# Seven block products for the last eight gate and up slices of layer 0's second half

## The chip, the cores and the metric

The kernel runs on one core of one Trainium2 chip. The metric is the device time of one execution in microseconds; the number to beat or to miss is the median of several executions.

## The reference

One inference step of a decoder with two layers, for 1024 prompt tokens and 8 sample tokens that share all weights. Cut to what matters here:

```python
def swiglu(h, w_gu, w_down):
    gate, up = jnp.split(h @ w_gu, 2, axis=-1)
    return (jax.nn.silu(gate) * up) @ w_down

# in run_trunk, per layer (layer 0: mixer A, layer 1: mixer B)
    h = h + rmsnorm(mix, g[1])
    h = h + rmsnorm(swiglu(rmsnorm(h, g[2]), w_gu[l], w_down[l]), g[3])
```

The model width is 1024 and the hidden width of the feed-forward network is 2816, 22 slices of 128. `w_gu` holds gate and up side by side. Results are wanted in float32 precision.

## The kernel before

The tokens are worked in two halves: g = 0 has 512 prompt tokens, g = 1 has 512 prompt tokens and the 8 sample tokens, 520 columns. Activations are kept transposed, 128 features by tokens. A float32 product is three matmuls: weights and activations are each split into a rounded high part and the rest (`split_w` and `split_to`: ScalarE casts, VectorE subtracts), and high x high, high x low and low x high are added up in PSUM. A half of 520 columns goes through TensorE as two pieces of 260, each with its own weight load.

`proj` is such a product for one slice of 128 outputs: for each of eight row blocks of 128 it issues 3 matmuls for each piece of 260, so 48 for the second half. `ffn.part(pi)` works through one of five groups of slices (`PARTS`: 5, 5, 4, 4 and 4). For each slice it runs `proj` for gate, `silu` (VectorE clips, ScalarE does exp, ln, exp, VectorE multiplies), `proj` for up, a multiplication and a split; then eight down projections over the group's slices add to the residual tile R.

The last stage of the program, layer 1's feed-forward for the second half (`ffn_w`), works otherwise. There gate and up of a slice are seen together as a 2 x 2 block matrix (rows 0 to 511 and 512 to 1023 of the weights; gate and up) times two blocks of 260 columns, and are got from seven products of 512 x 128 by 512 x 260 in place of eight, with sums of activations (`sums_w`) and sums of weight blocks. `gate_up_w` runs the seven products of one slice into four accumulators pa, pb, pc and pd; between products ScalarE copies one accumulator, negated, into another, and VectorE adds and subtracts (`gt`). It uses ScalarE's Silu itself, which lies in another table than exp and ln. The weight sums are made in DRAM by `weight_sums`: eight transfers a group, issued on GpSimd's queue, some of them accumulating, each held back by a token (a ScalarE copy of one column, then a GpSimd copy), so that they are spread over time.

Tiles come from pools with a fixed number of buffers: `wraw` (5) and `wspl` (5) for raw and split weights, `bpool` (7) for attention's temporary tiles, `apool` (8), `cpool` (4), and in PSUM `mmp` (2 tiles of 2 banks), `smp` (3 banks) and `nsp` (1). The main program weaves generators together by step counts, and the tile framework then sets each engine's order by its own estimate of when operands are ready. SP's queue carries the weight loads in one order, GpSimd's queue the sums and the gathers of cached keys and values.

The stages that the prediction speaks of, by the times of the trace: layer 0's first memory attention and output projection (some 240 to 350 us), the first half's `f0.part(4)` of layer 0 (some 765 to 835), the second half's parts 2, 3 and 4 of layer 0 (1191 to 1396), the second attention of layer 1 (some 1520 to 1935), its output projection (1935 to 1984), and layer 1's blocked feed-forward (2098 to 2382).

Of the kernel before, what the change touches and what calls it, by code (L numbers as in the profile page):

```python
# [24 lines left out]
def tile_decoder(  # L25
# [167 lines left out]
    def sv(ap, g):  # L193
        return ap[:, :G] if g == 0 else ap.rearrange("p (a n) -> p a n", a=2)

    def split_w(W, k0, nk, m0):
        out = []
        for a in range(0, nk, 4):
            n = min(4, nk - a)
            raw = wraw.tile([P, 4, P], F32, tag="w", name=nm("w"))  # L200
            nc.sync.dma_start(
                raw[:, :n, :],
                W[(k0 + a) * P : (k0 + a + n) * P, m0 : m0 + P].rearrange("(k p) m -> p k m", p=P),
            )
            ws = wspl.tile([P, 2, 4, P], F32R, tag="ws", name=nm("ws"))
            nc.scalar.copy(ws[:, 0, :n, :], raw[:, :n, :])  # L206
            nc.vector.tensor_sub(ws[:, 1, :n, :], raw[:, :n, :], ws[:, 0, :n, :].bitcast(F32))  # L207
            for i in range(n):
                out.append((ws[:, 0, i, :], ws[:, 1, i, :]))
        return out  # L210
# [90 lines left out]

    def sums_w(xs, ops):

# [27 lines left out]

    def YT():
        return xpool.tile([P, 2, NG[1]], F32R, tag="x0", name=nm("y"))
# [172 lines left out]

    def gate_up_w(l, f, ops, spl, raws, pair=None):

# [14 lines left out]
        def split(src):  # L523
            w = spl()
            nc.scalar.copy(w[:, 0, :], src)  # L525
            nc.vector.tensor_sub(w[:, 1, :], src, w[:, 0, :].bitcast(F32))  # L526
            return w

# [10 lines left out]

        pa, pb, pc, pd = (Q(i) for i in range(4))  # L540
        product(pa, 0, True)
# [88 lines left out]
    htok, done = [], []  # L630

    PARTS = [(0, 5), (5, 5), (10, 4), (14, 4), (18, 4)]

    class ffn_w:


        def __init__(self, l, x, plain):
            self.g, self.l, self.x, self.ops, self.plain, self.n, self.r, self.pi = 1, l, x, [], plain, 0, 0, 0
            self.R = self.acc = None
            self.half, self.mids = [], {}  # L640
            self.sums = sums_w(x, self.ops)

# [22 lines left out]
        def gate_up(self, pi, j0=0, j1=None):  # L665
# [3 lines left out]
            for j in range(j0, nf if j1 is None else j1):  # L669
                self.pi = pi  # L670
                if f0 + j < self.plain:
                    mt, ins = gate_up_q(l, f0 + j, self.x)
                    mids.append(mt)
                    with tc.issue_after(ins.ins):
                        for _ in range((1, 2, 1, 0)[j]):
                            next(self.sums, None)
                else:
                    pair = pairs[j // 2] if self.block(pi) and j < 4 else None
                    mids.append(gate_up_w(l, f0 + j, self.ops, self.spl, self.raws, pair))
                yield  # L680
# [214 lines left out]
    class ffn:  # L895
        def __init__(self, g, l, xt, rows=False):
            self.g, self.l, self.xt, self.rows = g, l, xt, rows
            self.R = self.acc = None

        def part(self, pi):  # L900
# [4 lines left out]
            mids = []  # L905
            for j in range(nf):
                pg = proj(g, w_gu[l], 0, ND, (f0 + j) * P, self.xt)
                sg = silu(None, pg, g)
                pu = proj(g, w_gu[l], 0, ND, DFF + (f0 + j) * P, self.xt)
                nc.vector.tensor_mul(sv(sg, g), sv(sg, g), pv(pu, g))  # L910
# [3 lines left out]
                self.now = sg[:, 0:1]  # L914
                yield
            if pi == 0:
                self.R = R_one()
            if last:
                self.acc = small([P, WID], tag="st", bufs=3)
            for m in range(ND):  # L920
                ps = proj(g, w_down[l], f0, nf, m * P, mids)
                evac_raw(g, self.R, ps, m, self.acc, pi == 0, last)
                self.now = self.R[m][:, 0:1]
                if m % 2:
# [844 lines left out]
    for blk in range(2):  # L1769
# [25 lines left out]
    weave((a1.core(), 22), (f0.part(0), 9), (down_sums(1, (1, 2, 3), lambda: f0.now), 24))  # L1795
    a1.open()
# [74 lines left out]
```

## Time and profile before

| | before |
|---|---|
| median of 3 runs | 2419.36 us (2418.62 to 2421.4) |
| the profiled execution | 2420.43 us, its span 2418.7 us |
| TensorE matmuls busy | 2395.5 us, 15411 instructions |
| weight loads busy | 2132.5 us |
| VectorE busy | 1602.8 us |
| ScalarE busy | 1241.3 us |
| GpSimd busy | 140.5 us |
| moved by DMA | 369.25 MB, 153 GB/s in the mean |
| stage 1191 to 1403 us | 212 us: TensorE 212.00, VectorE 105.11, ScalarE 85.84 busy; DMA share 0.83, 215 GB/s |

The engines are named PE (TensorE), PEld (its weight loads), DVE (VectorE), ACT (ScalarE), POOL (GpSimd) and SP (the queue that issues most loads). A row's "L220" is line 220 of the kernel. "Idle before <- X" says what ended the idle time in front of an instruction. PE's busy time is modelled and can reach its whole stretch without the array being at its peak, so it is read together with what PE waited for.

### The profile page before, as it was taken

The numbers are of one execution on the slowest core, as the hardware profiler recorded it, in microseconds if no ns is written. First come the engines' busy times: TensorE is split into PE (matmuls) and PEld (weight loads), VectorE is DVE, ScalarE is ACT, GpSimd is POOL, SyncE is SP. The second block draws the span as 40 slices with busy tenths as digits, with TensorE's granted clock in tenths as the row PEclk, the third lists the DMA queues.
The fourth block names the chain that finished last, engine by engine and source line by source line (L and its number), as shares of the span: only waits on it lengthen the run. The fifth ranks groups of instructions, "written<-read, shape, count | busy, mean of one in ns | idle before, by whom it ended". The sixth has DMA issues, their size and how long they took to land.

```text
span 2418.7 us, 40898 instructions
## 1 busy us (share of the span) xinstructions
PE 2395.5 (99%) x15411; PEld 2132.5 (88%) x15411; DVE 1602.8 (66%) x2792; ACT 1241.3 (51%) x2472; POOL 140.5 (6%) x215
## 2 busy tenths in 40 slices
PE   8999999999999999999999999999999999999998
PEld 6888998888877888999999989887787797999998
DVE  5777566765865677555544585877687648857885
ACT  5558554544444445555433454555454445565665
POOL 3000001200000000011111100121000000000000
PEclk9999999999999999999999999999999999999999
DMA  6353255884733445456778966644453334365652
GB/s 188 103 163 106 73 159 141 193 217 131 217 109 96 135 150 183 123 134 151 183 196 215 245 181 200 190 135 124 131 182 93 95 119 126 121 191 176 182 175 75
DMA packets 499224, 369.25 MB, mean 153 GB/s; under 512 B 19757, under 2 KB 444314, under 8 KB 499026
## 3 DMA queue, kind: packets, MB, share of 16 engines
q1 hardware_dynamic: 476008, 307.87, 42.7%
q0 software_dynamic: 22912, 58.73, 10.4%
q8 instruction: 121, 1.98, 0.3%
q14 instruction: 77, 0.63, 0.1%
q10 hardware_dynamic: 106, 0.04, 0.0%
HBM read 336.74 MB, written 80.15 MB: 172 GB/s over the span
## 4 chain that ended last, share of the span: by engine, by line
PE 91%; issue 4%; DVE 3%; ACT 1%; DMA 0%; POOL 0%; SPq 0%; DVEq 0%; POOLq 0%; ACTq 0%
PE mm L220 63%; PE q L535 7%; PE q L714 2%; PE q L493 2%; PE mm L1225 2%; PE s L1064 1%; PE q L778 1%; PE s L1023 1%; PE s L1408 1%; PE mm L977 1%; PE mm L1000 1%; PE q L862 1%; PE s L1583 1%; PE s L1622 1%; PE s L1050 1%
## 5 line engine op out<-in xcount | busy, mean ns | idle before, releaser
L220 PE MATMUL mm<-x,ws 128*128 128x260 f32 (+1 forms) x7776 | 1327.0, 329 | 0.5 <-DVE x L228 0.3
L220 PEld LDWEIGHTS mm<-x,ws 128*128 128x128 f32 x7776 | 1148.6, 188 | 140.1 <-issue 3.2
L206 ACT CAST ws<-w 128x512 fp32r<-128x512 f32 (+1 forms) x672 | 398.0, 593 | 648.2 <-PE mm L220 561.6
L207 DVE TENSOR_TENSOR ws<-w,ws 128x512 fp32r<-128x512 f32 (+1 forms) x672 | 438.2, 656 | 222.3 <-ACT ws L206 213.2
L220 PE MATMUL mm<-m,ws 128*128 128x512 f32 (+1 forms) x2112 | 391.0, 342 | 0.0
L220 PEld LDWEIGHTS mm<-m,ws 128*128 128x128 f32 x2112 | 323.5, 188 | 45.5 <-issue 2.1
L526 DVE TENSOR_TENSOR ws<-w,ws 128x512 fp32r<-128x512 f32 x126 | 86.6, 691 | 46.6 <-ACT ws L525 44.4
L535 PE MATMUL q<-y,ws 128*128 128x260 f32 x864 | 112.9, 283 | 0.0
L535 PEld LDWEIGHTS q<-y,ws 128*128 128x128 f32 x864 | 107.5, 188 | 0.0
L426 DVE TENSOR_TENSOR r<-r,mm 128x512 f32<-128x512 f32 (+1 forms) x96 | 66.0, 688 | 59.5 <-PE mm L220 58.1
L525 ACT CAST ws<-w 128x512 fp32r<-128x512 f32 x126 | 77.8, 618 | 47.7 <-PE q L535 15.3
L260 DVE TENSOR_SCALAR t<-mm 128x512 f32<-128x512 f32 (+1 forms) x74 | 51.2, 692 | 60.8 <-PE mm L220 60.7
L264 DVE TENSOR_TENSOR t<-t,t 128x512 f32<-128x512 f32 (+1 forms) x66 | 45.8, 693 | 68.1 <-ACT t L263 68.1
L910 DVE TENSOR_TENSOR t<-t,mm 128x512 f32<-128x512 f32 (+1 forms) x66 | 45.4, 689 | 67.4 <-PE mm L220 67.3
L535 PE MATMUL q<-x,ws 128*128 128x260 f32 x648 | 86.7, 283 | 0.0
L535 PEld LDWEIGHTS q<-x,ws 128*128 128x128 f32 x648 | 81.7, 189 | 0.0
L621 POOL COPY mk<-rr 128x1 f32<-128x1 f32 x64 | 29.6, 462 | 735.3 <-ACT rr L620 735.3
L290 DVE TENSOR_TENSOR st<-st,n 128x512 f32<-128x512 f32 (+1 forms) x91 | 62.2, 691 | 2.7 <-ACT n L289 1.5
L227 ACT CAST m<-t 128x512 fp32r<-128x512 f32 (+1 forms) x76 | 47.4, 624 | 26.0 <-DVE t L910 19.5
L261 ACT ACTIVATE t<-t 128x512 f32<-128x512 f32 (+1 forms) x66 | 42.1, 637 | 34.1 <-DVE t L260 29.9
L1161 POOL DMA_INDIRECT c<-in_cache_sb_k,pidx x16 | 20.0, 1250 | 608.9 <-DMA out_sbv_prompt<-c 427.2
L228 DVE TENSOR_TENSOR m<-t,m 128x512 fp32r<-128x512 f32 (+1 forms) x76 | 52.6, 692 | 2.3 <-ACT m L227 1.1
(385 smaller groups left out, 2889.2 us busy)
## 6 DMA issues: line engine op xcount, KB each, us to landing
w<-in_w_gu SPq DMA_DIRECT2D x334, 256.0 KB
w<-in_w_down SPq DMA_DIRECT2D x156, 256.0 KB
w<-in_w_in_a SPq DMA_DIRECT2D x80, 256.0 KB
wsum<-in_w_gu POOLq DMA_DIRECT2D x18, 1024.0 KB, 9.4
w<-wsum SPq DMA_DIRECT2D x72, 256.0 KB
w<-in_w_o SPq DMA_DIRECT2D x64, 256.0 KB
dsum<-in_w_down POOLq DMA_DIRECT2D x18, 512.0 KB, 6.6
w<-in_w_mem_kv SPq DMA_DIRECT2D x32, 256.0 KB
```

The costliest lines, as they stand in the source:

```text
L206: nc.scalar.copy(ws[:, 0, :n, :], raw[:, :n, :])
L207: nc.vector.tensor_sub(ws[:, 1, :n, :], raw[:, :n, :], ws[:, 0, :n, :].bitcast(F32))
L220: nc.tensor.matmul(ps[:, a, : PW[g]], wt, xt[k][:, xi, o : o + PW[g]], start=(k == 0 and wi == 0), stop=(k == nk - 1 and wi == 2),)
L228: nc.vector.tensor_sub(dst[1], src, dst[0].bitcast(F32))
L260: nc.vector.tensor_scalar(sv(x, g), pv(ps, g), -44.0, None, op0=ALU.max)
L290: nc.vector.tensor_add(acc[:, :n], acc[:, :n], t[:, :n])
L426: nc.vector.tensor_add(dst, dst, pv(ps, g))
L493: nc.tensor.matmul(pp[a][:, :h], wt, xt[k][:, xi, a * h : (a + 1) * h], start=(k == 0 and wi == 0), stop=(k == ND - 1 and wi == 2),)
L525: nc.scalar.copy(w[:, 0, :], src)
L526: nc.vector.tensor_sub(w[:, 1, :], src, w[:, 0, :].bitcast(F32))
L535: nc.tensor.matmul(ps[:, :h], w[:, wj, k * P : (k + 1) * P], x[:, xi, :], start=(first and k == 0 and wi == 0), stop=(k == 3 and wi == 2), ...
L714: nc.tensor.matmul(acc[i][q][:, :h], w[:, wj, o : o + P], x[:, xi, :], start=(first and t == 0 and wi == 0), stop=(t == 1 and wi == 2), sk ...
```

## The change

The second half's feed-forward of layer 0 runs slices 14 to 21 (parts 3 and 4, `FIRST = 14`) through `gate_up_w`. Its four accumulators come from the pools that are open there: pa and pd from `smp`, pb and pc as the two halves of one `mm` tile. Raw block weights lie in `bpool`, split ones in `wspl` and `cpool`, the sums of activations in `apool`. The sums are made beside slices 10 to 12. Silu's table is loaded in slice 14, and exp's and ln's again before part 4's down projection.

The weight sums for the two groups (16 transfers) are issued early: 7 while the first memory attention of layer 0 runs, 5 in the output projection behind it, 4 in `f0.part(4)`. Of layer 1's 40 transfers 16 stay where they were, 10 (24 before) stay beside the second half's parts 2 to 4, 8 go beside the second attention of layer 1 and 6 beside its output projection. The token now reads the newest split weight tile (`now`) in place of `sg` or R.

```diff
+        def quads(self):
+            two = mmp.tile([P, 2, 512], F32, tag="mm", name=nm("mm"))
+            return S(), two[:, 0, :], two[:, 1, :], S()
...
             for j in range(nf):
+                if f0 + j >= self.plain:
+                    mids.append(gate_up_w(
+                        l, f0 + j, self.ops, self.spl,
+                        lambda: B()[:, :512].rearrange("p (k m) -> p k m", m=P), self.quads,
+                    ))
+                    yield
+                    continue
                 pg = proj(g, w_gu[l], 0, ND, (f0 + j) * P, self.xt)
...
+                with tc.issue_after(ins.ins):
+                    for _ in range({4: 1, 3: 2, 2: 1}.get(self.plain - f0 - j, 0) if self.plain < NF else 0):
+                        next(self.sums)
                 yield
...
+            if last and self.plain < NF:
+                with tc.issue_after(done[-1].ins):
+                    nc.scalar.preload_act_table_set("natural_log_exp_and_others")
...
-    weave((a0.mem(), 8), (a1.fq(), 8))
+    here = lambda: now[0]
+    ws = weight_sums(0, (3, 4), here)
+    weave((a0.mem(), 8), (a1.fq(), 8), (islice(ws, 7), 7))
     o0 = out_proj(0, 0, M)
-    drain(o0.mm(a0.xo))
+    weave((o0.mm(a0.xo), 8), (islice(ws, 5), 5))
...
-    drain(f0.part(4))
+    weave((f0.part(4), 8), (ws, 4))
...
-    f1 = ffn(1, 0, o1.x)
-    ws = weight_sums(1, range(5), lambda: f1.now, 4)
+    f1 = ffn(1, 0, o1.x, FIRST)
+    ws = weight_sums(1, range(5), here, 4)
     weave((chain(b0.sb(), b0.mem()), 24), (chain(f1.part(0), f1.part(1)), 18), (islice(ws, 16), 17))
-    weave((chain(f1.part(2), f1.part(3), f1.part(4)), 24), (ws, 24))
+    weave((chain(f1.part(2), f1.part(3), f1.part(4)), 24), (islice(ws, 10), 10))
...
+        (chain(iter(range(20)), islice(ws, 8)), 32),
     )
     o1 = out_proj(1, 1, A, True)
-    drain(o1.mm(b1.xo))
+    weave((o1.mm(b1.xo), 8), (ws, 6))
```

What this does to the order, at three places. First TensorE at slice 14. Before, the gate projection of the slice stands there as one run: eight row blocks `x`, six matmuls each, into one `mm` tile:

```order
L220 MATMUL mm_12721<-x_9192,ws_12713 128x260 x6
L220 MATMUL mm_12721<-x_9196,ws_12713 128x260 x6
L220 MATMUL mm_12721<-x_9236,ws_12713 128x260 x6
L220 MATMUL mm_12721<-x_9240,ws_12713 128x260 x6
L220 MATMUL mm_12721<-x_9281,ws_12718 128x260 x6
```

Now, from the end of product 4 of slice 14 (into pb) to the start of product 6; `mm_12867` holds pb and pc, `s_13005` and `s_13006` are pa and pd of slice 15:

```order
L539 MATMUL mm_12867<-a_12454,ws_12944 128x260 x3
L539 MATMUL s_13005<-x_9280,ws_13009 128x260 x3
L539 MATMUL s_13005<-x_9284,ws_13009 128x260 x3
L539 MATMUL s_13005<-x_9324,ws_13009 128x260 x3
L539 MATMUL s_13005<-x_9328,ws_13009 128x260
L539 MATMUL mm_12867<-x_9369,ws_12965 128x260 x3
L539 MATMUL mm_12867<-x_9373,ws_12965 128x260 x3
L539 MATMUL mm_12867<-x_9413,ws_12965 128x260 x3
L539 MATMUL mm_12867<-x_9417,ws_12965 128x260 x3
L539 MATMUL s_13005<-x_9328,ws_13009 128x260 x2
L539 MATMUL s_13006<-a_12122,ws_13027 128x260 x3
L539 MATMUL mm_12867<-a_12121,ws_12983 128x260 x6
```

Ten matmuls of slice 15 have moved in front of product 5 (`x_9369` and on) and five in front of product 6 (`a_12121`). The first matmul of product 5 waits for VectorE, as does the first of product 6.

Second, SP's queue near the start of part 3, where the block weights (`b`, two of gate or up and then sums) and the loads of the down projections (`w`) now share it:

```order
L523 DMA b_13007<-in_w_gu 128x4x128
L523 DMA b_13025<-wsum_2332 128x4x128
L203 DMA w_13420<-in_w_down 128x4x128
L523 DMA b_13042<-wsum_2333 128x4x128
L203 DMA w_13451<-in_w_down 128x4x128
L203 DMA w_13487<-in_w_down 128x4x128
L523 DMA b_13060<-in_w_gu 128x4x128
```

The loads of part 3's down projection, `w_13420` and on, have moved between the block weights of slice 15, since the five tiles of `wraw` are free while gate and up use `bpool`.

Third, GpSimd's queue behind the stage. Before, the last sums of layer 1 stood in front of the remaining gathers of keys:

```order
L624 DMA wsum_13649<-in_w_gu 512x512
L621 COPY mk_14274<-rr_14272 128x1
L626 DMA wsum_13651<-wsum_13649 512x512
L621 COPY mk_14347<-rr_14345 128x1
L624 DMA wsum_13651<-in_w_gu 512x512
L1161 DMA c_16438<-in_cache_sb_k,pidx 128x512 x2
```

Now the moved sums (here the first of the 14) come behind the last gather of values:

```order
L1191 DMA c_17516<-in_cache_sb_v,pidx 128x512 x2
L1191 DMA c_17627<-in_cache_sb_v,pidx 128x512 x2
L1191 DMA c_17715<-in_cache_sb_v,pidx 128x512 x2
L625 COPY mk_18463<-rr_18461 128x1
L628 DMA wsum_14233<-in_w_gu 512x512
```

The sums have moved from ahead of the gathers to behind all of them, and the first gathers of keys, which before stood ahead of all of layer 1's sums, now come after the eighth of the ten sums that stay beside this stage.

More of the change, by code (lines that the diff above doesn't have):

```diff
@@ L194, in sv @@
         return ap[:, :G] if g == 0 else ap.rearrange("p (a n) -> p a n", a=2)
+    now = [None]
     def split_w(W, k0, nk, m0):
@@ L207, in split_w @@
             nc.vector.tensor_sub(ws[:, 1, :n, :], raw[:, :n, :], ws[:, 0, :n, :].bitcast(F32))
+            now[0] = ws[:, 0, 0, 0:1].bitcast(F32)
             for i in range(n):
@@ L505, in gate_up_q, with gate_up_w @@
         return mt, last
-    def gate_up_w(l, f, ops, spl, raws, pair=None):
+    def gate_up_w(l, f, ops, spl, raws, quads, pair=None):
         h, n = PW[1], NG[1]
@@ L526, in split @@
             nc.vector.tensor_sub(w[:, 1, :], src, w[:, 0, :].bitcast(F32))
+            now[0] = w[:, 0, 0:1].bitcast(F32)
             return w
@@ L538, in product @@
                     )
-        pa, pb, pc, pd = (Q(i) for i in range(4))
+        pa, pb, pc, pd = quads()
         product(pa, 0, True)
@@ L630, in tile_decoder @@
     htok, done = [], []
+    FIRST = 14
     PARTS = [(0, 5), (5, 5), (10, 4), (14, 4), (18, 4)]
@@ L640, in __init__ @@
             self.half, self.mids = [], {}
-            self.sums = sums_w(x, self.ops)
+            self.sums = sums_w(x, self.ops, Y0)
         def spl(self):
@@ L678, in gate_up @@
                     pair = pairs[j // 2] if self.block(pi) and j < 4 else None
-                    mids.append(gate_up_w(l, f0 + j, self.ops, self.spl, self.raws, pair))
+                    mids.append(gate_up_w(
+                        l, f0 + j, self.ops, self.spl, self.raws, lambda: [Q(i) for i in range(4)], pair
+                    ))
                 yield
@@ L895, in tile_decoder, with __init__, spl @@
     class ffn:
-        def __init__(self, g, l, xt, rows=False):
-            self.g, self.l, self.xt, self.rows = g, l, xt, rows
+        def __init__(self, g, l, xt, plain=NF):
+            self.g, self.l, self.xt, self.plain = g, l, xt, plain
             self.R = self.acc = None
+            self.ops, self.n = [], 0
+            self.sums = sums_w(xt, self.ops, lambda: A(F32R))
+        def spl(self):
+            self.n += 1
+            if self.n % 8 in (1, 4, 6):
+                return cpool.tile([P, 2, 512], F32R, tag="c", name=nm("ws"))
+            return wspl.tile([P, 2, 512], F32R, tag="ws", name=nm("ws"))
+        def quads(self):
+            two = mmp.tile([P, 2, 512], F32, tag="mm", name=nm("mm"))
+            return S(), two[:, 0, :], two[:, 1, :], S()
         def part(self, pi):
@@ L1789, in tile_decoder @@
     weave((chain(a0.gate(), a0.merge()), 8), (start(1, x1), 14))
-    weave((a0.mem(), 8), (a1.fq(), 8))
+    here = lambda: now[0]
+    ws = weight_sums(0, (3, 4), here)
+    weave((a0.mem(), 8), (a1.fq(), 8), (islice(ws, 7), 7))
     o0 = out_proj(0, 0, M)
-    drain(o0.mm(a0.xo))
+    weave((o0.mm(a0.xo), 8), (islice(ws, 5), 5))
     weave((o0.finish(), 17), (chain(a1.v(), a1.qm(A)), 8))
     f0 = ffn(0, 0, o0.x)
-    weave((a1.core(), 22), (f0.part(0), 9), (down_sums(1, (1, 2, 3), lambda: f0.now), 24))
+    weave((a1.core(), 22), (f0.part(0), 9), (down_sums(1, (1, 2, 3), here), 24))
     a1.open()
```

10 lines of the change are left out of this document (5 added, 5 removed).

## The prediction

> **What bounds the kernel now.** I read the page first, then the waits of PE, then the chain that ended last, then PE's timeline around the changed stage.
>
> ```profile
> span 2418.7 us, 40898 instructions
> PE 2395.5 (99%) x15411; PEld 2132.5 (88%) x15411; DVE 1602.8 (66%) x2792; ACT 1241.3 (51%) x2472; POOL 140.5 (6%) x215
> ```
>
> PE is busy 99% of the span, but its ends are modelled, so this alone proves little. The view of PE's waits does better: engine and line, what they waited for, total us, times, longest.
>
> ```profile
> PE s L145 <- DMA prow<-in_hg_norm: 7.7, 1, 7.7
> PE s L1610 <- DVE b L1604: 3.0, 9, 0.5
> ...
> PE mm L977 <- DVE memt L228: 0.2, 1, 0.2
> ```
>
> These are ten rows whose totals add up to about 15 us, half of it before the first matmul. In the chain of waits (start, duration, engine, line, count) the stage that the change touches is one unbroken row, and so are the stages of layer 1 that already run the block products (L535):
>
> ```profile
> 1191.49 209.81 PE mm L220 x1730
> ...
> 2143.56 50.48 PE q L535 x420
> ...
> 2290.64 40.42 PE q L535 x336
> ```
>
> So here PE alone sets the time: a matmul taken out of this stage is worth its whole pace, as long as nothing new makes PE wait. Everything else is either hidden or becomes such a wait.
>
> **The matmuls.** PE's timeline in the stage (start, duration, count):
>
> ```profile
> 1257.66 46.09 PE L220 MATMUL mm<-x,ws 128*128 128x260 f32 x384
> 1303.60 23.20 PE L220 MATMUL mm<-m,ws 128*128 128x260 f32 x192
> 1326.64 46.09 PE L220 MATMUL mm<-x,ws 128*128 128x260 f32 x384
> 1372.56 23.20 PE L220 MATMUL mm<-m,ws 128*128 128x260 f32 x192
> ```
>
> The x384 rows are gate and up of slices 14 to 17 and 18 to 21 (4 slices of 96 matmuls). From start to start they take 1303.60 - 1257.66 = 45.94 and 1372.56 - 1326.64 = 45.92 us, 119.6 ns a matmul. Afterwards a slice has 7 products x 4 x 3 = 84 matmuls of the same 260 columns, 336 for four slices. The chain's last L535 row is that very thing: four slices, 336 matmuls, 40.42 us (120.3 ns each). Each part gains 45.93 - 40.42 = 5.5 us, both parts **11.0 us**. The other new PE work is nil: the operand sums are made on DVE and ACT.
>
> **Waits that the shared PSUM tile adds.** In layer 1 the accumulators pb and pc have banks of their own. Here they are the two halves of one `mm` tile, and in the new order the first matmul of product 5 (into pc) waits for DVE, as the first of product 6 (into pb) does: the former for L557, which reads pb, the latter for L559, which reads pc. The order fills the two places with 8 to 10 and with 5 matmuls of the next slice (or of the down projection). How long must a fill be? One slice of layer 1, on PE, DVE and ACT (what is L557, L559 and L561 now was L553, L555 and L557 there):
>
> ```profile
> 2306.36 1.59 PE L535 MATMUL q<-y,ws 128*128 128x260 f32 x12
> 2307.79 1.61 PE L535 MATMUL q<-x,ws 128*128 128x260 f32 x12
> 2309.24 1.62 PE L535 MATMUL q<-y,ws 128*128 128x260 f32 x12
> ```
>
> ```profile
> 2307.55 0.69 DVE L526 TENSOR_TENSOR ws<-w,ws 128x512 fp32r<-128x512 f32 x1 [0.65 <-ACT ws L525]
> 2308.16 0.42 DVE L553 TENSOR_TENSOR t<-t,q 128x260 f32<-128x260 f32 x1
> 2308.64 0.69 DVE L526 TENSOR_TENSOR ws<-w,ws 128x512 fp32r<-128x512 f32 x1
> 2309.43 0.43 DVE L555 TENSOR_TENSOR t<-q,t 128x260 f32<-128x260 f32 x1
> ```
>
> ```profile
> 2309.96 0.42 ACT L557 ACTIVATE n<-t 128x260 f32<-128x260 f32 x1
> ```
>
> Product 5's slots end at 2309.24; L555 starts at 2309.43, ends at 2309.86, and the instruction that waits for it starts at 2309.96: 0.72 us from the last slot to the release. Five matmuls cover 0.60, so 0.12 us stays open per slice. Product 4's slots end at 2307.79; L553 starts 0.37 later behind a split, plus 0.42 and 0.10: 0.89 us, covered by 0.96 to 1.20. With one more split of 0.69 in front it would be 1.58, and 0.38 stays open; I take a fifth of that, 0.07. Together 0.19 us x 8 slices = **1.5 us**. The ends: nothing, and with no cover at all (0.72 + 0.89) x 8 = 12.9 us.
>
> **Supply of the block products.** Busy time in stretches (span; PE, PEld, DVE, ACT, POOL; granted clock, DMA share, GB/s), first of the changed stage, third of layer 1's four slices:
>
> ```profile
> 1191.00:1237.00 46.00, 46.00 (x385) 45.94 (x384) 22.54 (x33) 20.99 (x37) 6.76 (x9) 1.00 0.61 166
> 1367.00:1378.00 11.00, 11.00 (x93) 11.00 (x93) 6.13 (x9) 5.76 (x10) 1.58 (x2) 1.00 1.09 305
> 2290.00:2331.00 41.00, 41.00 (x343) 41.00 (x342) 31.60 (x63) 26.72 (x58) 0.00 (x0) 1.00 0.61 183
> ```
>
> In layer 1 the same products leave DVE 31.60 and ACT 26.72 busy of 41.00, with PE never idle; the new slices have less DVE work (no sums for a blocked down projection). The weights need 7 x 256 KB in 10.1 us, 182 GB/s, and ten weight sums of 1 MB over some 200 us add 51: 233 GB/s. Before, PE went on unhindered at 305 GB/s and a DMA share of 1.09. I cost the supply at **nothing**. Its cover is depth: 7 raw tiles and 9 split tiles. For a whole raw tile's round 7 x 1.44 = 10.1 us is allowed:
>
> ```profile
> L526 DVE TENSOR_TENSOR ws<-w,ws 128x512 fp32r<-128x512 f32 x22 | 15.2, 692 | 7.7 <-ACT ws L525 7.3
> L525 ACT CAST ws<-w 128x512 fp32r<-128x512 f32 x21 | 13.0, 617 | 5.9 <-PE q L535 3.4 <-ACT ws L525 1.1 <-PE q L714 0.8
> ```
>
> ```profile
> wsum<-in_w_gu POOLq DMA_DIRECT2D x18, 1024.0 KB, 9.4
> ...
> wsum<-in_w_gu POOLq DMA_DIRECT2D x6, 256.0 KB, 4.8
> ```
>
> Cast and split take 1.3 us; the nearest transfer of 256 KB whose landing the page shows takes 4.8. 6.1 us fits.
>
> **Operand sums.** Per pair of k: 12 DVE and 4 ACT instructions of 260 columns, four times.
>
> ```profile
> L563 DVE TENSOR_TENSOR n<-n,n 128x260 f32<-128x260 f32 x4 | 1.7, 424 | 0.0
> L227 ACT CAST ys<-n 128x260 fp32r<-128x260 f32 x6 | 2.5, 409 | 1.4 <-DVE n L563 1.3
> ```
>
> 48 x 0.424 = 20.4 us of DVE, 16 x 0.409 = 6.5 of ACT, in part 2, where DVE is idle 23 of 46 us while gate and up run. Nothing, while that holds. If the largest group (two pairs, 10.2 us) stood whole ahead of the DVE instruction that frees an `mm` bank, PE would use up the other bank's 48 x 0.120 = 5.7 us and wait 4.4. I take 0.
>
> **Silu's table.** Two table loads are added on ACT, one in slice 14, one before part 4's down projection.
>
> ```profile
> L765 ACT ACT_TABLE_LOAD x1 | 1.3, 1283 | 0.0
> ```
>
> 2 x 1.28 = 2.6 us if bare; split tiles stand eight products (11 us) ahead, so 0. The Trainium skill (ScalarE: Activation LUTs, What ACT_TABLE_LOAD costs) counts a drain of about 1.38 us on top, 2.66 a switch; by it a bare pair would cost 5.3 us instead of 2.6, and the sum is the same while the splits are ahead. The row here shows no idle time before the load.
>
> **Weight sums.** Sixteen POOL transfers are new (12 while layer 0's first memory attention and output projection run, 4 beside the first half's last part); of layer 1's 40, 14 move from this stage to the second attention of layer 1 (8) and to its output projection (6).
>
> ```profile
> 300.00:345.00 45.00, 44.93 (x274) 39.58 (x273) 25.58 (x41) 20.84 (x38) 0.00 (x0) 1.00 0.56 171
> 765.00:835.00 70.00, 70.00 (x329) 57.78 (x328) 38.91 (x57) 31.68 (x52) 0.00 (x0) 1.00 0.41 124
> 1935.00:1984.00 49.00, 49.00 (x388) 47.42 (x387) 16.65 (x25) 20.27 (x37) 0.00 (x0) 1.00 0.42 130
> ```
>
> Five in 45 us add 117 to 171 GB/s, four in 70 add 60 to 124, six in 49 add 128 to 130: at most 288, under the 305 that cost PE nothing. The gathers of cached keys now stand behind this stage's blocks, since both use the pool `cpool`, but in the new order all gathers of values come before the moved sums on POOL. If PE had to sit out all 30 transfers at 305 GB/s, it would be 30 x 3.4 = 103 us; the row at share 1.09 lies nearest, so 0. The sums' tokens are ACT copies of one column:
>
> ```profile
> L620 ACT COPY rr<-t x36: 184/187/192, 391.1 to 1374.0; 128x1 f32<-128x1 f32 x36
> ```
>
> Sixteen more are 3 us of an ACT that is half idle; reading a weight split instead of `sg` or R, they wait for no other engine.
>
> **Sum.** 2420.43 us (the profiled execution) - 11.0 + 1.5 = 2410.9. The median of the runs shown, 2419.36, lies 1.07 lower: **2409.9, said as 2410**.
>
> **Rivals.** First, *the fills don't cover*: DVE gets late in its queue, and products 5 and 6 wait. For it: the first matmuls of both name DVE, and DVE has splits of 0.69 us on both sides of L557 and L559. Against: the fills match the latencies above to a tenth. Bare, it gives 2419.4 - 11.0 + 12.9 = 2421.3; half bare 2414.8. Second, *slower: raw tiles run short*. Layer 1's blocks draw on two pools of raw tiles, these on the seven of `bpool` alone, and SP's queue is in order. It decides once a round takes longer than 10.1 us, so once a load lands later than 8.8 us; if it lands as late as the 1 MB transfers, 9.4 us, little happens (10.7 / 7 = 1.53 instead of 1.44, 56 x 0.09 = 5 us, less what the head start hides). To be slower than before by 0.2% it must eat 9.5 + 4.8 us: 56 x 0.255, a round of 11.9, landing at 10.6 us; at 14 us, 56 x (15.3 / 7 - 1.44) = 42, hence 2452. Against: 256 KB at 4.8, and less traffic than before. Third, *the moved and new sums disturb*: keys come late or ACT's tokens block on POOL, 5 to 15 us in the attention stages, 2415 to 2425. Against: PE's few waits there today, and POOL idle where they go. That fewer matmuls are not issued can be left out: the order shows them.
>
> **How the numbers follow.** A difference under about 0.2% (4.8 us) can't be told from no change here; the bounds are 2414.5 and 2424.2. Forecast (2408 to 2412.5): 0.72. Fills don't cover: 0.16, of it 0.07 still under 2414.5 and 0.09 within. Raw tiles: 0.06, slower. Sums: 0.06, of it 0.05 within, 0.01 slower. Faster 0.79, same 0.14, slower 0.07. The low end is the whole 11.0 without waits, 2408.4, less 1.4 for the spread of runs; the high end 2418 leaves out the raw tiles, half of the sums and a third of the first rival, 0.14.
>
> **What would show it.** Right: a row of 336 block matmuls taking 40.5 to 42 us in place of each 45.9, PE's waits on L557 and L559 small, and the down rows still 23.0 us. Wrong: idle time before L539 put down to DVE on every slice (first rival); ACT's cast L528 waiting for DMA into `b` (second); new PE waits between 1400 and 1990 us or near 240 to 350 (third).

## The result and the profile after

The changed kernel takes **2429.41 us** in the median of 7 runs (2426.66 to 2430.59), against 2420.23 for the kernel before in the same comparison (2418.62 to 2421.4): a ratio of 1.0036, with a 95% interval of 1.0027 to 1.0046. The forecast was 2410.0 with a range of 2407 to 2418. It was wrong in its sign: 9 us slower instead of 9 us faster. One of the five executions of the fastest kernel below took 6050.98 us; the other four took 2409.13 to 2411.29, and no reading rests on it.

The page after, its busy times:

```profile
PE 2393.6 (99%) x15315; PEld 2127.0 (88%) x15315; DVE 1626.5 (67%) x2872; ACT 1264.4 (52%) x2546; POOL 161.3 (7%) x247
```

The 96 matmuls are gone (15411 before), but PE's busy time has fallen by 1.9 us, not by 11, and the span has grown by 9.6, from 2418.7 to 2428.3 us. The view of PE's waits has two large rows that were not there before:

```profile
PE mm L223 <- DVE r L429: 6.7, 1, 6.7
PE mm L223 <- ACT m L230: 3.3, 1, 3.3
```

PE's timeline of the stage shows where they are:

```profile
1192.36 43.63 PE L223 MATMUL mm<-x,ws 128*128 128x260 f32 x362
1235.83 6.16 PE L223 MATMUL mm<-m,ws 128*128 128x260 f32 x48
1248.67 19.70 PE L223 MATMUL mm<-m,ws 128*128 128x260 f32 x144 [6.69 <-DVE r L429]
1268.21 1.62 PE L539 MATMUL s<-x,ws 128*128 128x260 f32 x12
...
1316.38 22.82 PE L223 MATMUL mm<-m,ws 128*128 128x260 f32 x168 [3.33 <-ACT m L230]
1339.05 1.60 PE L539 MATMUL s<-x,ws 128*128 128x260 f32 x12
...
1404.52 5.70 PE L223 MATMUL mm<-x,ws 128*128 128x512 f32 x24
```

Both waits lie in a down projection (`mm<-m`), one at the end of part 2, where slices 10 to 13 still run the old way, and one at the end of part 3. From start to start, the down projection of part 2 takes 1268.21 - 1235.83 = 32.38 us (23.05 before), part 3 takes 70.84 (68.98 before), and part 4 65.47 (68.96 before). The whole stage, 1192.36 to 1404.52, has grown from 204.46 to 212.16 us. Without any loss it would have shrunk by 11.0, so it loses 18.7.

What held PE up at the end of part 2 is read from the other engines. ScalarE's timeline after:

```profile
1236.95 0.63 ACT L230 CAST m<-t 128x520 fp32r<-128x520 f32 x1 [0.30 <-DVE t L936]
1246.67 0.62 ACT L528 CAST ws<-b 128x512 fp32r<-128x512 f32 x1 [9.09 <-DMA b<-wsum]
1247.19 0.61 ACT L208 CAST ws<-w 128x512 fp32r<-128x512 f32 x1
...
1315.18 0.62 ACT L528 CAST ws<-b 128x512 fp32r<-128x512 f32 x1 [4.87 <-DMA b<-wsum]
```

VectorE's, at the same place:

```profile
1247.32 0.69 DVE L529 TENSOR_TENSOR ws<-b,ws 128x512 fp32r<-128x512 f32 x1 [9.01 <-ACT ws L528]
1247.93 0.69 DVE L429 TENSOR_TENSOR r<-r,mm 128x520 f32<-128x520 f32 x1
```

And the queues that issue transfers, SP's and then GpSimd's:

```profile
1232.71 5.06 SPq L203 DMA_DIRECT2D w<-in_w_down  x3
1237.87 2.66 SPq L523 DMA_DIRECT2D b<-wsum  x1
```

```profile
1231.46 1.05 POOL L628 DMA_DIRECT2D wsum<-in_w_gu  x1
```

Read from the bottom up: a block weight's sum for slice 14 is issued at 1237.87, behind three loads of the down projection that took 5.06 us to issue, 6.4 us after a weight sum of 1 MB had started. The chain of waits (start, duration) gives its landing as 8.78 us, and that of the block at part 3's end as 7.82:

```profile
1237.87 8.78 DMA b<-wsum
...
1307.29 7.82 DMA b<-wsum
```

ScalarE's cast of that block (L528) stands in its queue in front of the down projection's own cast (L208) and waits 9.09 us. VectorE's half of the split (L529) waits behind it, and behind that stands L429, which empties the `mm` tile that PE needs. So PE waits for a product that lies a whole down projection ahead. At 1315 another block does the like: L528 waits 4.87 us, and behind it in ScalarE's queue stands the cast of `m` (L230), which the running down projection multiplies.

Before, the transfers were no fewer. A window of the kernel before at the end of part 3 (PE; clock, DMA share, GB/s), and a row of its SP queue at the end of part 2:

```profile
1310.00:1315.00 5.00, 5.00 (x44) 1.00 1.12 229
```

```profile
1233.32 26.34 SPq L201 DMA_DIRECT2D w<-in_w_gu  x10
```

The DMA share was as high, and PE never idle. The second row is a run of single loads, some 2.9 us apart, that goes on past the end of the view (1262 us); the first is for slice 14, and the first matmul of that slice stands at 1257.66, 24 us after its issue. In the whole stage no cast of a gate, up or down weight waited for DMA.

A second loss hangs on the first. The windows of PE give, behind its busy time, the granted clock, the DMA share and GB/s:

```profile
1240.00:1245.00 5.00, 1.98 (x17) 1.00 1.02 266
1245.00:1250.00 5.00, 1.33 (x6) 0.68 0.70 193
1250.00:1255.00 5.00, 5.00 (x30) 0.64 0.81 239
...
1315.00:1320.00 5.00, 3.62 (x16) 0.50 0.31 81
1320.00:1325.00 5.00, 5.00 (x37) 0.81 0.64 206
```

After each wait the windows of 5 us show a granted clock of 0.50 to 0.81, for 5 to 10 us. The down projection of part 2 lost 32.38 - 23.05 = 9.33 us, of which 6.69 is the wait and 2.64, for the most part, the clock (the 144 matmuls from 1248.67 took 19.54 us where 144 x 0.120 = 17.28 was to be had); the 168 matmuls from 1316.38 took 22.67 us where 168 x 0.120 = 20.16 was to be had, so 2.51 more. The Trainium skill (TensorE: Matmul & The Clock Gate, Part 1: The HAM clock gate) says that an idle window of about 3.4 us halves the clock until PE has been busy for about as long. The trace agrees for the wait of 6.69 us; the one of 3.33 us, a little shorter than that window, was followed by the slower clock too, and waits of 1.0 and 1.2 us in the experiments were not.

The 18.7 us are thus 6.69 + 2.64 + 3.33 + 2.51 = 15.2 for the two waits and what follows them, and the remaining 3.5 us, some 0.45 a slice, lie in the eight slices.

Outside the stage, 1404.52 to 1945 us took 0.7 us more than before. An added 1.2 us before the stage (a cached value that PE waited for near 745) is missing in the first four experiments, which have the same program there and start the stage between 1190.66 and 1190.92; it is not counted.

### The profile page after: what moved, and what is told of

Its sections match the earlier page's. It is cut to its first block, busy times and chain, and to the rows that moved or that the text cites. A ratio compares the mean times of both kernels' runs of the same rounds, so it can differ in the third digit from the quotient of the medians.

```text
span 2428.3 us, 40981 instructions
## 1 busy us (share of the span) xinstructions
PE 2393.6 (99%) x15315; PEld 2127.0 (88%) x15315; DVE 1626.5 (67%) x2872; ACT 1264.4 (52%) x2546; POOL 161.3 (7%) x247
## 4 chain that ended last, share of the span: by engine, by line
PE 91%; DVE 4%; DMA 2%; ACT 2%; issue 1%; POOL 0%; SPq 0%; DVEq 0%; ACTq 0%
PE mm L223 59%; PE q L539 7%; PE q L721 2%; PE q L496 2%; PE mm L1255 2%; PE mm L539 2%; PE s L539 1%; PE q L785 1%; PE s L1094 1%; PE s L1053 1%; PE s L1438 1%; PE s L1613 1%; PE mm L1007 1%; PE mm L1030 1%; PE q L869 1%
## 5 line engine op out<-in xcount | busy, mean ns | idle before, releaser
L223 PE MATMUL mm<-x,ws 128*128 128x512 f32 (+1 forms) x7008 | 1234.7, 335 | 0.5 <-DVE x L231 0.2
L223 PEld LDWEIGHTS mm<-x,ws 128*128 128x128 f32 x7008 | 1056.5, 188 | 140.0 <-issue 3.4
L208 ACT CAST ws<-w 128x512 fp32r<-128x512 f32 (+1 forms) x640 | 378.1, 591 | 559.9 <-PE mm L223 472.7
L209 DVE TENSOR_TENSOR ws<-w,ws 128x512 fp32r<-128x512 f32 (+1 forms) x640 | 414.7, 652 | 208.5 <-ACT ws L208 204.9
L223 PE MATMUL mm<-m,ws 128*128 128x512 f32 (+1 forms) x2112 | 397.2, 345 | 10.0 <-DVE r L429 6.7
L529 DVE TENSOR_TENSOR ws<-w,ws 128x512 fp32r<-128x512 f32 x126 | 86.5, 691 | 46.9 <-ACT ws L528 43.9
L429 DVE TENSOR_TENSOR r<-r,mm 128x512 f32<-128x512 f32 (+1 forms) x96 | 66.0, 687 | 57.9 <-PE mm L223 56.7
L528 ACT CAST ws<-w 128x512 fp32r<-128x512 f32 x126 | 77.8, 618 | 47.8 <-PE q L539 15.3
L267 DVE TENSOR_TENSOR t<-t,t 128x512 f32<-128x512 f32 (+1 forms) x58 | 40.1, 691 | 53.1 <-ACT t L266 53.1
L263 DVE TENSOR_SCALAR t<-mm 128x512 f32<-128x512 f32 (+1 forms) x66 | 45.5, 689 | 44.3 <-PE mm L223 44.3
L936 DVE TENSOR_TENSOR t<-t,mm 128x512 f32<-128x512 f32 (+1 forms) x58 | 39.8, 686 | 50.3 <-PE mm L223 50.2
L528 ACT CAST ws<-b 128x512 fp32r<-128x512 f32 x56 | 34.4, 618 | 54.9 <-PE mm L223 22.3
L230 ACT CAST m<-t 128x512 fp32r<-128x512 f32 (+1 forms) x76 | 47.4, 623 | 26.2 <-DVE t L936 20.0
L529 DVE TENSOR_TENSOR ws<-b,ws 128x512 fp32r<-128x512 f32 x56 | 38.5, 691 | 31.5 <-ACT ws L528 30.9
```

What stands on the lines that cost most here:

```text
L223: nc.tensor.matmul(ps[:, a, : PW[g]], wt, xt[k][:, xi, o : o + PW[g]], start=(k == 0 and wi == 0), stop=(k == nk - 1 and wi == 2),)
L230: nc.scalar.copy(dst[0], src)
L429: nc.vector.tensor_add(dst, dst, pv(ps, g))
```

## The experiments

The diffs are against the changed kernel. The kernel before ran 2420.34 to 2420.51 us beside them.

**One part alone: the weight sums.** Gate and up as before; the sums, and where they stand, as in the change.

```diff
-    f1 = ffn(1, 0, o1.x, FIRST)
+    f1 = ffn(1, 0, o1.x)
```

> Changed: layer 0's gate and up run as before the change (no block products, no activation sums); all weight sums stay where the change put them, layer 0's 16 are made and not read. It is the cost of the sums alone. Queue theory: nothing in the stage of parts 2 to 4, since its loads go through wraw as before; what the trace shows outside the stage stays, 1.3 us by 1190 and 0.7 after 1404, so 2420.2 + 2 = about 2422. Traffic theory: 14 sums less in the stage and 30 elsewhere cost 5 us or more elsewhere, 2425 or more. If the sums are free: 2420.

2420.63 us, ratio 1.0001 (0.9991 to 1.001), and the stage took 204.47 us. Sixteen more transfers and fourteen moved ones cost nothing by themselves, with the old gate and up.

**One part undone: no sums beside the stage.** The ten that stay there go to the second attention of layer 1, which then has 18.

```diff
-    weave((chain(f1.part(2), f1.part(3), f1.part(4)), 24), (islice(ws, 10), 10))
+    weave((chain(f1.part(2), f1.part(3), f1.part(4)), 24))
...
-        (chain(iter(range(20)), islice(ws, 8)), 32),
+        (chain(iter(range(20)), islice(ws, 18)), 42),
```

> Changed: the ten weight sums of layer 1 that stay beside parts 2 to 4 go to the second attention of layer 1 (18 there). Queue theory: the loads land somewhat sooner, as one 1 MB transfer less runs beside them, but the early cast still waits behind a load that SP issues late; a stall of 3 to 6 us stays at the end of part 2, 2422 to 2428. Traffic theory: no 1 MB transfer in the stage, loads land in 3 to 5 us, both stalls go, 2414 to 2417. Shared-PSUM theory: 2427 to 2430.

2421.61 us, ratio 1.0004 (0.9995 to 1.0014): no gain as a whole, but the trace splits it. The stage took 198.23 us, 6.2 less than before. PE's timeline, ScalarE's and SP's, at the place of the first wait:

```profile
1241.69 17.52 PE L223 MATMUL mm<-m,ws 128*128 128x260 f32 x144 [1.20 <-DVE r L429]
```

```profile
1239.69 0.62 ACT L528 CAST ws<-b 128x512 fp32r<-128x512 f32 x1 [3.60 <-DMA b<-wsum]
```

```profile
1231.23 1.57 SPq L203 DMA_DIRECT2D w<-in_w_down  x3
1232.89 0.46 SPq L523 DMA_DIRECT2D b<-wsum  x1
```

And the chain, for the landing of that block's sum:

```profile
1232.89 6.77 DMA b<-wsum
```

The same cast waits 3.60 instead of 9.09 us. Of this difference of 5.5 us the smaller part is the landing, 6.77 instead of 8.78 us. The larger part is the issue: the three loads in front take 1.57 instead of 5.06 us to issue, so this one is issued 3.20 us before ScalarE is free for its cast (1232.89 and 1236.09), and with the sums 0.29 us after (1237.87 and 1237.58), which makes 3.5 us. The second wait is gone, and the clock stays at 1.00. What the stage won, the second attention lost: 547.35 us from the stage's end to 1936.44, against 539.64 before. Its windows (both of PE, this kernel's):

```profile
1800.00:1850.00 50.00, 49.56 (x248) 1.00 0.96 248
1850.00:1900.00 50.00, 46.38 (x233) 1.00 0.57 165
1900.00:1945.00 45.00, 42.80 (x255) 1.00 0.58 141
```

PE idles for 5.8 us behind a stretch with a DMA share near 1 (1.02 from 1750 to 1800); before, the share there was 0.25 to 0.67 and PE idled for 0.02 between 1850 and 1945. PE's largest waits there are in the prompt tokens' attention to the memory (L1080 and L1094 in `mem_attn`; 1.3 and 2.4 us the longest).

**The order on ScalarE.** The splits of layer 0's block weights are held until the last cast and subtraction of the down projection's weights have been placed, so that no early L528 can stand in front of them.

```diff
+            tail[0] = nc.scalar.copy(ws[:, 0, :n, :], raw[:, :n, :])
+            tail[1] = nc.vector.tensor_sub(ws[:, 1, :n, :], raw[:, :n, :], ws[:, 0, :n, :].bitcast(F32))
...
-            nc.scalar.copy(w[:, 0, :], src)
-            nc.vector.tensor_sub(w[:, 1, :], src, w[:, 0, :].bitcast(F32))
+            if l == 0:
+                with tc.issue_after(tail[0].ins), tc.issue_after(tail[1].ins):
+                    nc.scalar.copy(w[:, 0, :], src)
+                    nc.vector.tensor_sub(w[:, 1, :], src, w[:, 0, :].bitcast(F32))
...
```

> Changed: the casts and subtractions that split layer 0's block weights may no longer stand on ScalarE and VectorE ahead of the previous part's last down-projection split. Queue theory (a block weight's cast put early into ScalarE's queue waits for a load of 8 to 9 us, and the down projection's splits and evacuations behind it wait too): both PE waits, 6.7 us near 1242 and 3.3 near 1313, go, and with them the two stretches of 10 us or so at a lower granted clock (2.5 us each); 2429.4 - 15 = about 2414. Shared-PSUM theory (products 5 and 6 wait for VectorE): these waits are not touched, 2426 or more. Traffic theory (the sums' transfers make the loads late): the loads stay as late and PE waits at the start of slice 14 in place of the down projection, 2422 to 2429.

2422.73 us, ratio 1.0004 (0.9995 to 1.0014): 7 us better than the change, but no gain. The stage took 206.17 us, 6.0 less than in the change, and 5.5 of them lie in part 3, which takes 65.31 us (70.84 in the change): its wait of 3.33 us is gone, and the slower clock behind it. The down projection of part 2 still takes 31.96 us (32.38 in the change). Its one wait has become two that are together as long. PE and then ScalarE and VectorE:

```profile
1244.53 11.77 PE L224 MATMUL mm<-m,ws 128*128 128x260 f32 x96 [1.56 <-DVE r L430]
1261.45 4.80 PE L224 MATMUL mm<-m,ws 128*128 128x260 f32 x24 [5.15 <-DVE r L430]
```

```profile
1242.52 0.62 ACT L209 CAST ws<-w 128x512 fp32r<-128x512 f32 x1 [6.83 <-DMA w<-in_w_down]
1258.76 2.18 ACT L531 CAST ws<-b 128x512 fp32r<-128x512 f32 x4 [10.42 <-DMA b<-wsum]
```

```profile
1259.40 1.29 DVE L532 TENSOR_TENSOR ws<-b,ws 128x512 fp32r<-128x512 f32 x2 [8.12 <-ACT ws L531]
1260.62 0.69 DVE L430 TENSOR_TENSOR r<-r,mm 128x520 f32<-128x520 f32 x1
```

No block stands in front of the first wait: now the down projection's own weights come 6.83 us late. In the second the order is still wrong: the hold binds the blocks' splits to the last split of the down projection's weights, not to its additions into R, so a block's subtraction (L532) still stands on VectorE ahead of L430. So the order of casts cost the wait of part 3; beside the sums the load that is wanted next landed late at the end of part 2 in either order. The range of the traffic theory holds the time, but PE waits inside the down projection and not at the start of slice 14, as it said.

**The shared PSUM tile.** Product 5 gets a bank of its own. The sum that product 5 completes in the new bank isn't the reference's; the instructions are the same in kind and number.

```diff
-            return S(), two[:, 0, :], two[:, 1, :], S()
+            return S(), two[:, 0, :], S(), S()
```

> Changed: accumulator pc gets a PSUM bank of its own, so product 5 no longer waits for the read of pb, nor product 6 for the read of pc. Shared-PSUM theory: the eight slices get back 0.5 us or more each, 4 to 13 us, 2416 to 2425. Queue theory: the two stalls and their slow clock stay; the slices get back 0.2 to 0.5 us each, 2425.5 to 2428.

2427.08 us, ratio 1.0026 (1.0015 to 1.0036). Both waits in the down projections stay (6.53 and 5.90 us). Part 4, which has neither, takes 64.16 us from its first block product to its end, against 65.47: 1.3 us for four slices. The shared tile is a real cost, but not the cause of the loss.

**The ten sums early, alone and with the other edits.** They go beside parts 2 and 3 of the first half's feed-forward, and from there on there are four kernels: the sums alone, with the hold, with a bank for product 5, and with both. In the last two, product 5 starts from zero in its bank, and the copied part waits in SBUF and is added there, so that nothing of the computation changes.

```diff
+    wt = weight_sums(1, range(5), here, 4)
...
-    weave((chain(a1.merge(), a1.mem()), 12), (a1.mem_sample(), 22), (chain(f0.part(2), f0.part(3)), 16))
+    weave(
+        (chain(a1.merge(), a1.mem()), 12), (a1.mem_sample(), 22), (chain(f0.part(2), f0.part(3)), 16),
+        (islice(wt, 10), 10),
+    )
...
-        nc.scalar.activation(pc[:, :h], pb[:, :h], AF.Copy, scale=-1.0)
+        nc.scalar.activation(dt[:, :h] if l == 0 else pc[:, :h], pb[:, :h], AF.Copy, scale=-1.0)
...
+            nc.vector.tensor_sub(dt[:, :h], dt[:, :h], dt[:, h:n])
+            product(pc, 5, True)
+            nc.vector.tensor_add(gt[:, :h], pc[:, :h], dt[:, :h])
...
```

The sums alone:

> The ten layer-1 weight sums of the stage go to the first half of layer 0 (beside parts 2 and 3 of the feed-forward block of the first 512 tokens), where the DMA engines had a share of 0.29 to 0.42 before; the second attention of layer 1 keeps its 8. Theory (the block weights' loads land late beside the 1 MB sums): the stage takes 198 us as without sums, the second attention 540 to 541 us, so 2413 to 2415. Rival (loads and casts queue the wrong way round, whatever the traffic): the stalls at the ends of parts 2 and 3 stay, 2420 or more. Second rival: the early place costs what the second attention lost with 18 sums (7.7 us): about 2421, with new waits between 700 and 850 us.

With the hold:

> As the kernel with early sums, and the splits of layer 0's block weights held behind the last cast and difference of the down projection's weights. Theory (late landings are the main cause, the order on ScalarE makes each of them stop the down projection): the 1.2 us wait that is left without sums goes, 2412 to 2415. Rival (holding only moves the wait to the first products of slice 14, since loads are then behind): equal to the kernel with early sums or up to 3 us slower.

With the bank:

> As the kernel with early sums, and product 5 in a PSUM bank of its own (it starts from zero there, and the negated copy of pb lies in SBUF and is added by one more DVE instruction per slice). Theory: the shared tile costs about 0.3 to 0.4 us a slice, 8 slices, so 2.4 to 3.2 us less than with early sums alone: 2410 to 2412. Rival (the waits come from product 6, which must wait for the sum that reads pb, wherever pc lies): less than 1 us.

With both:

> Early sums, held splits and product 5 in a bank of its own together. If the three gains add: 2409 to 2412, the sum that was predicted. If holding the splits costs at the first products, 2412 to 2415.

| | us | ratio to before (95%) | stage |
|---|---|---|---|
| before | 2420.34 | | 204.46 |
| sums early | 2418.46 | 0.9994 (0.9985 to 1.0004) | 198.34 |
| and hold | 2417.96 | 0.9991 (0.9981 to 1.0) | 197.90 |
| and bank | 2415.66 | 0.9982 (0.9972 to 0.9991) | 195.50 |
| and both | 2414.51 | 0.9976 (0.9966 to 0.9985) | 193.71 |

The stage does as expected in all four, and the four times miss what the theory expected by 2.5 to 3.7 us (the last lies in its second range, the one for a cost of the hold, but its stage shows no such cost). The second rival of the first expectation holds in kind, at a little over half of its price: it put that kernel at 2421. The traces of the two kernels with the hold are of executions 2.2 and 6.4 us above their medians, and what these lose lies ahead of the stage, which starts at 1197.68 and 1198.78. PE's waits between 690 and 770 us in the kernel with the early sums:

```profile
PE ns L1160 <- DVE c L1158: 2.3, 1, 2.3
PE mm L223 <- DVE r L429: 0.9, 1, 0.9
```

Before, there are none; in the changed kernel the first was 1.4. L1158 and the line above it work on a cached value that SP loads at that point; VectorE waits 4.57 us for the load there, and 1.52 before. The place that the DMA share made look free has loads that are wanted at once.

**The ten sums elsewhere.** They go between 790 and 950 us: four beside the end of the first half of layer 0, six beside layer 1's first queries. Four gathers of cached keys are issued there too (923.97 to 929.77 in the kernel before), but PE waits for none of them, before or after.

```diff
-    weave((f0.finish(True), 9), (o1.mm(a1.xo, 1, 5), 4))
+    wt = weight_sums(1, range(5), here, 4)
+    weave((f0.finish(True), 9), (o1.mm(a1.xo, 1, 5), 4), (islice(wt, 4), 4))
...
-    weave((b0.heads(), 8), (o1.finish(), 17))
+    weave((b0.heads(), 8), (o1.finish(), 17), (islice(wt, 6), 6))
...
```

With hold and bank:

> As the kernel with all three edits, but the ten sums stand between 790 and 950 us (4 beside the end of the first half of layer 0, 6 beside the query projections of layer 1's first attention), where no cached keys or values are gathered. Theory (1 MB sums cost where SP's loads are needed at once, the cached values at 735 to 750 us as the block weights in the stage): the stage takes 194 us as with all three edits, and the 3 to 5 us of idle PE between 730 and 750 us go back to 0 to 1.4, so 2409 to 2412. Rival (a fixed price of the extra traffic, wherever it is): new waits between 790 and 950 us, 2414 or more.

With the bank, without the hold:

> As the kernel before it, without holding the splits. Theory: the stage takes 195 to 196 us, so 1 to 2 us more than with the hold, 2410 to 2414. Rival (without sums in the stage the order of casts costs nothing): equal within 0.5 us.

With nothing else altered:

> The change, with nothing altered but the place of ten weight sums: between 790 and 950 us instead of beside parts 2 to 4. Theory (sums beside the new block loads are the main cause; the shared tile costs 2.8 us on top and the order of casts 1): the kernel with the own bank and these sums took 2410.4, so 2412.5 to 2414. Rival (the earlier differences came from other edits, not from the sums): 2418 or more.

| | us | ratio to before (95%) | stage |
|---|---|---|---|
| sums moved, nothing else | 2413.70 | 0.9972 (0.9961 to 0.9983) | 198.03 |
| and bank | 2410.42 | 0.9958 (0.9941 to 0.9974) | 195.39 |
| and bank and hold | 2409.56 | 0.9957 (0.9941 to 0.9973) | 193.12 |

All three came out as expected. Only the place of ten transfers turns 9.2 us slower into 6.75 us faster, 15.7 us between the medians of the two kernels; the bank adds 3.3 us. The hold shortens the stage by 2.3 us in the trace, but the medians differ by only 0.9, and the intervals do not part them. In the kernel with the sums moved and nothing else the early cast L528 still stands ahead of L208 at the end of part 2; it is the wait for its load that is shorter. ScalarE's waits for block sums in the stage (total us, times, longest), in the changed kernel and then in this one:

```profile
ACT ws L528 <- DMA b<-wsum: 15.4, 3, 9.1
```

```profile
ACT ws L528 <- DMA b<-wsum: 4.8, 2, 3.4
```

A median landing says little of this: for the blocks' sums it is 3.1 us in this kernel and 3.2 in the one with the hold, whose stage has the ten sums beside it; for the down projection's loads it is 3.2 and 4.2. What differs is a few loads at the ends of parts 2 and 3. The stage of the fastest kernel, in PE's timeline:

```profile
1189.29 43.63 PE L225 MATMUL mm<-x,ws 128*128 128x260 f32 x362
1232.76 23.20 PE L225 MATMUL mm<-m,ws 128*128 128x260 f32 x192
1296.02 23.14 PE L225 MATMUL mm<-m,ws 128*128 128x260 f32 x192
1359.29 23.28 PE L225 MATMUL mm<-m,ws 128*128 128x260 f32 x192
1382.41 5.70 PE L225 MATMUL mm<-x,ws 128*128 128x512 f32 x24
```

From down projection to down projection it takes 63.26 and 63.27 us, where the kernel before took 68.99 and 68.96: 5.7 us less in each, and every down row is back at 23.1 to 23.3.

## Why the prediction was wrong

- **What bounds the kernel**: right. PE sets the time of the stage; every microsecond that it did not wait was a gain.
- **The matmuls, -11.0 us**: right. With the waits taken away, the two parts gain 5.7 us each, 11.4 in all. That the kernel then stands at 2409.56, where the sum of the terms was 2409.9, is partly luck: it is not the kernel that was forecast, and it has no shared tile, for which the sum holds 1.5 us.
- **The shared PSUM tile, +1.5 us**: the right mechanism, too small. The bank is worth 2.8 us beside the early sums (2418.46 to 2415.66) and 3.3 beside the moved ones (2413.70 to 2410.42), or 0.35 to 0.41 us a slice instead of 0.19. In the kernel with the sums moved and nothing else, the view of the weight loads' waits in the stage names L557, the reader of pb; with the bank the row is gone:

```profile
PEld mm L539 <- DVE t L557: 1.2, 6, 0.2
```

  It shows 1.2 of the 3.3 us. The rest lies at the same places, in gaps too short for that view. PE's timeline at product 5 of one slice of that kernel:

```profile
1286.72 1.12 PE L539 MATMUL s<-x,ws 128*128 128x260 f32 x8
1287.82 1.73 PE L539 MATMUL mm<-x,ws 128*128 128x260 f32 x12
1289.38 0.64 PE L539 MATMUL s<-x,ws 128*128 128x260 f32 x4
```

  From start to start the eight matmuls take 1.10 us where 8 x 0.120 = 0.96 was to be had, and the twelve of product 5 take 1.56 instead of 1.44: 0.26 us, and product 6 of the slice adds 0.19 in the same way. The prediction had 0.07 and 0.12 for the two places.
- **The supply of the block products, nothing**: this is the step that failed. The prediction counted the cover in tiles (7 raw, 9 split) and in a steady round of 10.1 us, and took a landing of 4.8 us. What counted was the moment at the end of parts 2 and 3 at which three queues meet. ScalarE's queue holds casts of blocks in front of the casts that the running down projection needs; SP's queue holds the load for such a cast behind loads that take their time; and a 1 MB sum at the same moment makes issue and landing slower. At the end of part 2 the landing was 8.78 us with the sums beside it and 6.77 without, and the issue came 3.5 us later against its cast. None of this is in the average, which the prediction had put at 233 GB/s, under the 305 that PE had lived with. That row was no evidence, since the kernel before issued its loads far ahead: in the same stretch its DMA share reached 1.12 without a wait. The change did not shorten the way from a load to its matmul: the block that stopped PE was issued at 1237.87, and slice 14's first product stands at 1268.21, 30 us later, against 24 before. It took away the distance from the load to its cast: ScalarE was free for that cast 0.29 us before the load was issued, and at the end of part 3 only 3.0 us after.
- **The price of a wait**: left out. A wait of 6.69 us cost 9.33, and one of 3.33 cost 5.84; the excess is for the most part the lower clock that PE was granted afterwards.
- **The operand sums and Silu's tables, nothing each**: no wait of PE named either in any run, and the fastest kernel has both. A table load in the changed kernel took 1.28 us (from 1273.66), and ScalarE's next instruction started at 1274.95, so the bare price was 1.28 a load and not more.
- **The weight sums, nothing**: right for the sixteen new and the fourteen moved (the run of the sums alone), but only for the dose: with ten more, the second attention lost 7.7 us, and beside the first half of layer 0 they brought waits of 2.3 and 0.9 us. The third rival was a true mechanism that the change stayed short of.
- **The rivals**: the second one named the row that came, ScalarE's L528 waiting for DMA into `b`, and the right sign. But it looked for a round that is too long all the time, at every slice, put "against" it that a landing takes 4.8 us and that there was less traffic, and gave it 0.06. Two landings of 7.8 and 8.8 us at the wrong moment were enough.

The causes were parted like this: gate and up the old way with the same sums, no loss; the new gate and up without sums beside them, no wait above 1.2 us in the stage; the casts in order with the sums, still a loss. It takes the sums and the new supply together. Of the supply, the order on ScalarE made the wait of part 3 (the hold alone takes it away, as moving the sums alone does), and at the end of part 2 the loads come late in either order. What stays open is why SP's issues become slow there (see the last section), and what a hold that also binds the additions into R would have saved beside the sums: no run tried it.

## What to carry to other kernels

Cover for a weight load is a distance in time from issue to use, and it is to be followed at the boundaries of a stage, through each in-order queue between: the queue that issues the load, the engine that first touches it, and whatever stands behind that instruction. A DMA share that costs nothing in one kernel says little of another that reads closer to its deadline; background transfers belong where no load is urgent, and a share of 0.3 to 0.4 does not prove that none is. And a wait of PE of 3.3 us or more is to be priced with the slower clock that follows, 2 to 3 us each time here; a wait of 2.3 us sometimes.

## What the runs showed of the hardware

SP's issue of a load is itself slow at times, and a 1 MB sum beside it is neither needed for that nor enough. The durations of such issues (least, median, most, in ns), first in the stage of the kernel before, then between 1230 and 1246 us in the changed kernel, then in the stage of the kernel with the sums moved:

```profile
L201 SPq DMA_DIRECT2D w<-in_w_gu x38: 367/368/368, 1193.5 to 1345.4; - x38
```

```profile
L203 SPq DMA_DIRECT2D w<-in_w_down x5: 368/368/3857, 1231.2 to 1245.0; - x5
```

```profile
L523 SPq DMA_DIRECT2D b<-wsum x32: 359/366/2556, 1222.6 to 1342.2; - x32
```

Before, 23 sums were issued in the stage, and none of the 62 loads of gate, up and down weights took above 368 ns to issue; they stood some 2.9 us apart. In the changed kernel one took 3857, 2.5 us behind the issue of a sum, and in the kernel with the hold one took 3652, just as far behind one. With no sum in the stage one still took 2556, the last of nine loads that SP issued one behind the other from 1229.61 on. So close succession goes with issues of over 2 us by itself, and with a sum beside it they are longer: the three loads of the down projection take 5.06 us with it and 1.57 without. Their tiles came free alike: VectorE's three subtractions that free them start 0.70 and 0.71 us before the first load and take 1.88 and 1.89. Whether this lies in the DMA engines or in the memory behind them, no run here shows. The Trainium skill (DMA: Bandwidth & Descriptors, Queues, rings and completion order) says that a DMA engine takes turns between its queues, a whole packet at a time; that fits the later landings beside a sum, while a slower issue does not follow from it.

The length of a wait alone does not decide whether the clock falls. Between 745 and 751 us PE waits 2.30 us in the kernel with the early sums and 2.31 us at the same place in the one that also has the hold. In the first the granted clock stays at 1.00; in the second the window from 750 to 755 us shows 0.66.
